# Layer 0's first feed-forward product with seven seven-product pairs instead of five, its weights and operands in order of use, and the groups around it divided

## The chip, the cores and the metric

The kernel runs on one core of one Trainium2 chip. The metric is the time of one execution in microseconds, as the device takes it; the time before is 2281.53 us, the median of three runs (2276.98 to 2283.56). A core has a matrix engine (TensorE, PE in the rows), a vector engine (DVE), a scalar engine (ScalarE, ACT), GpSimd (POOL) and SyncE (SP). Here SP issues the loads of weights, and POOL issues transfers that add one block of memory to another.

## The reference

Two layers of a recurrent trunk are computed on 512 time steps of width 1024, in single precision. Shortened:

```python
for i in range(DEPTH):                        # DEPTH = 2
    h = rmsnorm(x, norm1_g[i]);  z = h @ w_in[i] + b_in[i]
    # branch A: mLSTM with 4 heads; branch B: retention with 4 heads of q, k 256, v 512
    merged = sigmoid(gm) * (y_m @ w_bm[i]) + sigmoid(gr) * (y_r @ w_br[i])
    x = x + merged @ w_out[i]
    h2 = rmsnorm(x, norm2_g[i])
    x = x + square(relu(h2 @ w_ff1[i] + b_ff1[i])) @ w_ff2[i] + b_ff2[i]     # 1024 -> 4096 -> 1024
    h3 = rmsnorm(x, norm3_g[i])
    x = x + sigmoid(h3 @ w_pe_gate[i]) * (p[i] @ w_pe[i])
return rmsnorm(x, final_g)
```

## The kernel before

Activations lie transposed, features on the 128 partitions and the 512 time steps along the columns. Every product is made three times over: each operand is split into a high part and a low remainder, and high·high, high·low and low·high are summed (lines L502 to L504 for plain units, L557 to L559 for pairs). ScalarE makes the high part (L321), DVE the low one (L322), of weights as of activations.

A weight reaches TensorE in two forms. A **plain unit** ("T8") is one tile of 128 output columns: 24 matmuls of 512 columns, results named `l0f` in the feed-forward. A **pair** makes two such tiles by a seven-product scheme (Strassen's): the time steps are halved into 256 columns, and products P1 and P5 use the weight piece A, P6 and P2 piece B, P3 and P7 piece C, P4 piece D, twelve matmuls of 256 columns each, 84 in all. Its names are `l0f11` or `l0o10`, and its banks a, b and c. P4 is deferred: it runs inside the next unit, at the `flush()` behind that unit's P5 (or at the place that the unit has for it). The pieces A, B, C hold 1024 columns and D 512. They are sums of weight blocks. Most sums are made ahead in memory by POOL's adding transfers (L379), which are paced by a credit: each unit of work adds a share of its time (`SHARE`, from the third branch gate of layer 0 on `LATER`), each transfer takes off `STEP` = 1.13 us, and none is issued while the credit is negative. In layer 0 the sum in the second half of piece B of some groups and the one for D are made on DVE (for D, L484); in layer 1's first product all come from memory. Raw weights are loaded by SP into four buffers (`wr`), and the split pieces have three buffers; both are filled in one fixed order, the order of the units and within a unit that of `parts_of`: A, C, B, D.

The **feed-forward** has four groups b of 1024 hidden values. The first product of a group has four units "f" (b, p) of 256 hidden values: a pair where `FPAIRS` names it, else two plain units. What comes out is scaled on DVE (L1518), passed through relu and square on ScalarE (L1519, L1520) and split into quarters (`pair_quarters`: `hh`, `hl`, 128x768), and three sums of it on DVE (L652 to L654) are split as the last operand part (128x1024). The second product of the group has four pairs "o" (b, p), which use all four f units of their group; their products are added to `x` on DVE (L1554, L1556), and a bank is written again only behind such an addition. `ff_order` puts the first f unit of the next group between the last f unit of a group and its four o pairs. At the end of the feed-forward the embedding product (`l1pe`) takes this place, before `o30`.

In the retention branch, head after head, `attend` multiplies the decayed scores with the values in four slices j of 128 rows, slice j summing over j + 1 blocks of three matmuls. Before it lies the pair that makes the next head's key (`brk`), so that its deferred P4 is run at the `flush()` behind the first slice. This P4 needs a sum on DVE (L643) first.

A list scheduler with priorities sets the final order on each engine; queues are in order on SP and POOL.

## Time and profile before

| What | Value |
|---|---|
| runs, median (range) | 2281.53 us (2276.98 to 2283.56) |
| profiled execution, its span | 2280.06 us, 2278.3 us |
| granted TensorE clock | 0.999 |
| TensorE busy | 2263.4 us (99%) |
| DVE, ScalarE, POOL busy | 1747.5, 1281.5, 605.5 us |
| feed-forward of layer 0 | from about 757 to 1097 us |

Times of instructions are counted from the start of the span. A row of the timeline gives start, duration, engine, line, operation, the written tile, the tiles read, and in brackets the idle time ahead of it with the instruction that ended it. A window's row gives, for each engine, the busy time and in brackets the instructions, in the order PE, weight loads, DVE, ACT, POOL; then the granted clock, the busy share of the transfer engines and GB/s.

### The profile page before, as it was taken

The page shows a single profiled execution, that of the slowest core. Times are in us where ns is not written, and L with a number is a line of the kernel's source. Part 1 is how long each engine was busy: PE and PEld are TensorE (multiplying, and loading weights), DVE is VectorE, ACT ScalarE, POOL GpSimd, SP SyncE. Part 2 cuts the span into 40 slices and gives each one's busy share as a digit, 9 for nine tenths or more (in the row PEclk, how much of TensorE's full clock was granted, in tenths as well). Part 3 has the DMA queues.
Part 4 walks back from the last instruction along what each step waited for, and adds up shares of the span by engine and source line. Part 5 has one row for each costly group of instructions (what it writes and reads, how often), then busy time and mean ns, then how long its engine had stood idle before and what let it go on. Part 6 is the DMA issues. An engine that isn't in the chain of part 4 may idle for free.

```text
span 2278.3 us, 36390 instructions
## 1 busy us (share of the span) xinstructions
PE 2263.4 (99%) x13532; PEld 2009.3 (88%) x13532; DVE 1747.5 (77%) x2680; ACT 1281.5 (56%) x1881; POOL 605.5 (27%) x952
## 2 busy tenths in 40 slices
...
GB/s 215 189 192 176 246 224 223 222 232 216 236 231 267 222 229 228 238 238 222 227 220 197 185 178 244 240 210 223 239 216 219 248 265 217 256 239 231 249 159 60
DMA packets 185889, 499.32 MB, mean 219 GB/s; under 512 B 26400, under 2 KB 26784, under 8 KB 185712
## 3 DMA queue, kind: packets, MB, share of 16 engines
...
## 4 chain that ended last, share of the span: by engine, by line
PE 90%; DVE 5%; ACT 2%; issue 1%; DMA 1%; POOL 0%; SPq 0%; DVEq 0%; ACTq 0%; POOLq 0%
PE l0f L502 2%; PE l0f L503 2%; PE l0f L504 2%; PE l0br L502 1%; PE l0br L503 1%; PE l1br L502 1%; PE l1br L503 1%; PE l1br L504 1%; PE l0br L504 1%; DVE w_B L322 1%; PE l0pg L502 1%; PE l0pg L504 1%; PE l1bm L503 1%; PE l0bm L503 1%; PE l0bm L502 1%
## 5 line engine op out<-in xcount | busy, mean ns | idle before, releaser
L322 DVE TENSOR_TENSOR w<-wr,w 128x1024 fp32r<-128x1024 f32 (+1 forms) x193 | 234.3, 1217 | 47.6 <-ACT w L321 45.3
L321 ACT ACTIVATE w<-wr 128x1024 fp32r<-128x1024 f32 (+1 forms) x193 | 199.7, 1041 | 122.3 <-issue 28.5
L321 ACT ACTIVATE w_B<-wr 128x1024 fp32r<-128x1024 f32 x123 | 130.5, 1061 | 148.5 <-PE l1bm L504 13.1
L322 DVE TENSOR_TENSOR w_B<-wr,w_B 128x1024 fp32r<-128x1024 f32 x123 | 150.2, 1222 | 52.5 <-ACT w_B L321 52.3
L321 ACT ACTIVATE w_C<-wr 128x1024 fp32r<-128x1024 f32 x75 | 79.3, 1058 | 63.4 <-issue 9.5
L322 DVE TENSOR_TENSOR w_C<-wr,w_C 128x1024 fp32r<-128x1024 f32 x75 | 92.5, 1234 | 28.6 <-ACT w_C L321 28.6
L322 DVE TENSOR_TENSOR w_A<-wr,w_A 128x1024 fp32r<-128x1024 f32 x75 | 91.7, 1223 | 15.6 <-ACT w_A L321 14.6
L321 ACT ACTIVATE w_A<-wr 128x1024 fp32r<-128x1024 f32 x75 | 79.0, 1053 | 39.6 <-DMA wr<-wpairs 8.8
L321 ACT ACTIVATE w_t<-wr 128x1024 fp32r<-128x1024 f32 x56 | 59.4, 1060 | 62.7 <-PE l0g2va L610 6.3
L321 ACT ACTIVATE w_D<-wr 128x512 fp32r<-128x512 f32 x75 | 47.3, 631 | 67.3 <-DVE wr L484 18.3
L322 DVE TENSOR_TENSOR w_t<-wr,w_t 128x1024 fp32r<-128x1024 f32 x56 | 68.3, 1222 | 21.2 <-ACT w_t L321 20.6
L502 PE MATMUL l0f<-l0n2h,w 128*128 128x512 f32 x176 | 68.8, 391 | 0.0
L503 PE MATMUL l0f<-l0n2l,w 128*128 128x512 f32 x176 | 68.7, 390 | 0.0
L504 PE MATMUL l0f<-l0n2h,w 128*128 128x512 f32 x176 | 68.6, 390 | 0.0
L322 DVE TENSOR_TENSOR w_D<-wr,w_D 128x512 fp32r<-128x512 f32 x75 | 51.7, 689 | 14.1 <-ACT w_D L321 13.7
L379 POOL DMA_DIRECT2D s30t<-wpairs x24 | 16.8, 701 | 88.7 <-PE l1o20a L559 8.7
L504 PEld LDWEIGHTS l0f<-l0n2h,w 128*128 128x128 f32 x176 | 33.1, 188 | 6.9
L502 PEld LDWEIGHTS l0f<-l0n2h,w 128*128 128x128 f32 x176 | 33.1, 188 | 6.6
L503 PEld LDWEIGHTS l0f<-l0n2l,w 128*128 128x128 f32 x176 | 33.1, 188 | 6.5
L502 PE MATMUL l1f<-l1n2h,w 128*128 128x512 f32 x96 | 37.6, 392 | 0.0
L503 PE MATMUL l1f<-l1n2l,w 128*128 128x512 f32 x96 | 37.5, 390 | 0.0
L504 PE MATMUL l1f<-l1n2h,w 128*128 128x512 f32 x96 | 37.4, 390 | 0.0
...
## 6 DMA issues: line engine op xcount, KB each, us to landing
...
```

The source lines that it names most:

```text
L321: a = ac.activation(hi_ap, src, AF.Copy)
L322: return a, ve.tensor_sub(lo_ap, src, hi_ap.bitcast(F32))
L379: dma = gp.dma_start(piece(g, x, p, q), piece(g, MADE[x][a], p, q), max_dma_last_dim=4096, **kw)
L502: te.matmul(o, sh, mh, start=first, stop=False)
L503: te.matmul(o, sh, ml, start=False, stop=False)
L504: cur["mm"] = te.matmul(o, sl, mh, start=False, stop=last)
```

## The change

Five edits, made together:

1. `FPAIRS` of layer 0 names seven f units instead of five, so two units that were two plain ones each become pairs, and others change place: (0,2), (1,1), (1,2), (2,1), (2,2), (3,1), (3,2) for (1,1), (1,3), (2,1), (2,3), (3,1). Layer 1 keeps its ten.
2. Where the first f unit of the next group is plain, which is so for all three in layer 0 and none in layer 1, `ff_order` divides it: its first plain unit ("fa") goes ahead of two o pairs, its second one with the split of the operands ("fb") behind them, then come the other two.
3. Pieces of feed-forward pairs are split, and loaded, in the order A, B, C, D in which their products use them. Other pairs keep A, C, B, D.
4. `attend` begins with slice 1 where a deferred product is pending, and flushes behind that one: heads 0 and 2 of each layer.
5. `LATER` is .76 instead of .75. The adding transfers become 682 instead of 670.

```diff
--- before.py
+++ after.py
@@ -77,18 +77,21 @@
 SLACK = 64
 
 
-def ff_order():
+def ff_order(i):
 
     seq = [("f", 0, p) for p in range(4)]
     for b in range(3):
-        seq.append(("f", b + 1, 0))
-        seq += [("o", b, p) for p in range(4)]
+        o = [("o", b, p) for p in range(4)]
+        if (b + 1, 0) in FPAIRS[i]:
+            seq += [("f", b + 1, 0)] + o
+        else:
+            seq += [("fa", b + 1, 0)] + o[:2] + [("fb", b + 1, 0)] + o[2:]
         seq += [("f", b + 1, p) for p in range(1, 4)]
     return seq, [("o", 3, p) for p in range(4)]
 
 
 
-FPAIRS = (((1, 1), (1, 3), (2, 1), (2, 3), (3, 1)), ((0, 2), (1, 0), (1, 1), (1, 3), (2, 0), (2, 1), (2, 3), (3, 0), (3, 1), (3, 2)))
+FPAIRS = (((0, 2), (1, 1), (1, 2), (2, 1), (2, 2), (3, 1), (3, 2)), ((0, 2), (1, 0), (1, 1), (1, 3), (2, 0), (2, 1), (2, 3), (3, 0), (3, 1), (3, 2)))
 
 
 PRODUCTS = {"P1": ("A", 0, 0), "P5": ("A", 1, 4), "P2": ("B", 0, 2), "P6": ("B", 1, 5), "P3": ("C", 0, 6),
@@ -109,17 +112,22 @@
 HALVES = [(WIDE[x][0], u) for x, u in TURNS]
 
 SOON = ("w_in", 0, CGM + 2 * P)
-STEP, SHARE, LATER = 1.13, 0.75, 0.75
+STEP, SHARE, LATER = 1.13, 0.75, 0.76
 TIME = {"PAIR": (9.9, 3.9), "WIDE": (5.45, 2.7), "FULL": (9.9, 5.0)}
 
 
 def parts_of(u):
 
-    return {"PAIR": list(PIECE), "WIDE": HALVES}.get(u[0], [0])
+    pair = "ABCD" if u[0] == "PAIR" and is_ff(u[1]) else "ACBD"
+    return {"PAIR": list(pair), "WIDE": HALVES}.get(u[0], [0])
 
 
 
 READY = {"P1": 2, "P4": 2, "P5": 3, "P2": 4, "P6": 4, "P3": 4, "P7": 5}
+
+
+def is_ff(g):
+    return g[1][0] == "f"
 
 
 def is_wide(g):
@@ -237,15 +245,15 @@
         for kind, b, p in seq:
             if (b, p) in FPAIRS[i] and kind == "f":
                 pair(f"fp{b}", [q for c, q in FPAIRS[i] if c == b].index(p))
-            elif kind == "f":
-                t8("w_ff1", b * 1024 + 256 * p)
-                t8("w_ff1", b * 1024 + 256 * p + P)
+            elif kind[0] == "f":
+                for d in {"fa": (0,), "fb": (1,)}.get(kind, (0, 1)):
+                    t8("w_ff1", b * 1024 + 256 * p + d * P)
             else:
                 pair(f"ff{b}", p)
 
-    pairs(ff_order()[0])
+    pairs(ff_order(i)[0])
     u.append(("PE", 0))
-    pairs(ff_order()[1])
+    pairs(ff_order(i)[1])
     u.append(("PE", 1))
     full("w_pe_gate")
     return u
@@ -401,7 +409,10 @@
 
     order = [(n, x) for n, u in enumerate(units) for x in parts_of(u)]
     place = {x: k for k, x in enumerate(order)}
-    loads = [(n, x) for n, x in order if full(n) or x not in ("D", ("t4", 0), ("t4", 1))]
+    loads = []
+    for n, u in enumerate(units):
+        ls = "ACBD" if u[0] == "PAIR" and not has_t2(u[1]) else parts_of(u)
+        loads += [(n, x) for x in ls if full(n) or x not in ("D", ("t4", 0), ("t4", 1))]
     raws, pieces, kept = {}, {}, {}
     formed = {}
 
@@ -447,6 +458,14 @@
         at["prep"] += 1
         fill_raws()
 
+        g = units[n][1] if x in list("ABCD") else None
+
+        def t2_sum():
+            if not has_t2(g):
+                ve.tensor_tensor(raws[n, "B"][:, Q:], kept.pop((n, "A"))[:, Q:], raws[n, "C"][:, :Q], OP.add)
+
+        if x == "B" and is_ff(g):
+            t2_sum()
         w = Q if x == "D" else UN
         pl = cur["last"] if n >= NU - LAST else wpool
         kw = {"tag": "d", "bufs": 1} if x == "D" else {"tag": "l", "bufs": LAST} if pl is not wpool else {
@@ -459,7 +478,7 @@
         out_ = [both[:, o + a * w:o + a * w + w] for a in range(1 if gates else 2)]
         r = formed.pop((n, x), None)
         if r is None:
-            r = raws.pop((n, x))
+            r = raws[n, x]
         if gates:
             z = out_[0]
             gp.memset(z.bitcast(F32), 0.0)
@@ -472,13 +491,13 @@
         else:
             in_order("prep", *split(r[:, :w], *out_))
         pieces[n, x] = out_
-        if full(n) or not wide and x in ("A", "C") and has_t2(units[n][1]):
+        if x == "C" and not is_ff(g):
+            t2_sum()
+        raws.pop((n, x), None)
+        if full(n) or x == "C" or x == "A" and has_t2(g):
             pass
         elif x == "A" or wide and x[0] == "t2":
             kept[n, x] = r
-        elif x == "C":
-
-            ve.tensor_tensor(raws[n, "B"][:, Q:], kept.pop((n, "A"))[:, Q:], r[:, :Q], OP.add)
         elif x == "B":
 
             ve.tensor_tensor(r[:, :Q], r[:, :Q], r[:, Q:], OP.add)
@@ -858,13 +877,14 @@
 
     def attend(nm, pt, vh, vl, c0, n, num, each=None):
         ph, pl, offs = pt
-        for j in range(NT):
+        slices = (1, 0, 2, 3) if later else range(NT)
+        for j in slices:
             o = ps(f"{nm}a{j}")
             for i in range(j + 1):
                 s = slice(offs[i] + (j - i) * P, offs[i] + (j - i + 1) * P)
                 mm3(o[:, :n], ph[:, s], pl[:, s], vh[i][:, c0:c0 + n], vl[i][:, c0:c0 + n], i == 0, i == j)
             ac.activation(num[:, j, :], o[:, :n], AF.Copy)
-            if j == 0:
+            if j == slices[0]:
                 flush()
             if each:
                 each(j)
@@ -1507,7 +1527,9 @@
         cur["own"] = "new"
         hid = {}
 
-        def ff1(b, p):
+        begun = []
+
+        def ff1(b, p, part=False):
 
             nm = f"l{i}f{b}{p}"
             hid[b, p] = [cur["ff"].tile([P, 7 * S], F32R, name=f"l{i}h{a}{b}{p}", tag=f"h{a}", bufs=5) for a in "hl"]
@@ -1537,9 +1559,17 @@
                 evac(1, o1)
             else:
                 evac(0, o)
-                evac(1, t8(n2.act, f"{nm}1"))
-            pair_quarters(st, *hid[b, p])
-            pair_operand(nm, st, *hid[b, p])
+
+            def second():
+                if b or p:
+                    evac(1, t8(n2.act, f"{nm}1"))
+                pair_quarters(st, *hid[b, p])
+                pair_operand(nm, st, *hid[b, p])
+
+            if part:
+                begun.append(second)
+            else:
+                second()
 
         def tile3(c):
             n3.tile(c, x[c])
@@ -1578,10 +1608,13 @@
 
             run_pair(f"l{i}o{b}{p}", [parts(k) for k in range(4)], done)
 
-        first, rest = ff_order()
+        first, rest = ff_order(i)
         for kind, b, p in first:
             if kind == "o":
                 ff2(b, p)
+                continue
+            if kind == "fb":
+                begun.pop()()
                 continue
             if (b, p) == (3, 1):
                 pth, ptl = [cur["ff"].tile([P, 2, T], F32R, name=f"l{i}pt{a}", tag=f"h{a}", bufs=5) for a in "hl"]
@@ -1589,7 +1622,8 @@
                     t = tmp(f"l{i}ptr{k}")
                     nc.scalar.dma_start(t, ins["pT"][i, k])
                     split(t, pth[:, k, :], ptl[:, k, :])
-            ff1(b, p)
+            ff1(b, p, kind == "fa")
+        assert not begun
         ns_pool.release()
         n2_pool.release()
         n3_pool = phase(f"n3{i}", act_side)
```

What moves on the engines, at three places. First TensorE in layer 0's retention, head 0, around the deferred product of head 1's key (`l0r1brka`, piece `w51_D`); `l0r0a0` and `l0r0a1` are slices 0 and 1. Before:

```order
L559 MATMUL l0r1brka_3918<-l0xsh6_1371,w51_C_3890 128x256
L502 MATMUL l0r0a0_4045<-l0r0vh0_2629,l0r0ph_3747 128x512
L503 MATMUL l0r0a0_4045<-l0r0vl0_2633,l0r0ph_3747 128x512
L504 MATMUL l0r0a0_4045<-l0r0vh0_2629,l0r0pl_3748 128x512
L502 MATMUL l0r0a1_4081<-l0r0vh0_2629,l0r0ph_3747 128x512
L557 MATMUL l0r1brka_3918<-l0xnh1_1052,w51_D_3935 128x256
L558 MATMUL l0r1brka_3918<-l0xnl_386,w51_D_3935 128x256
```

With the change:

```order
L578 MATMUL l0r1brka_3921<-l0xsh6_1374,w51_C_3893 128x256
L521 MATMUL l0r0a1_4048<-l0r0vh0_2632,l0r0ph_3750 128x512
L522 MATMUL l0r0a1_4048<-l0r0vl0_2636,l0r0ph_3750 128x512
L523 MATMUL l0r0a1_4048<-l0r0vh0_2632,l0r0pl_3751 128x512
L521 MATMUL l0r0a1_4048<-l0r0vh1_2633,l0r0ph_3750 128x512
L522 MATMUL l0r0a1_4048<-l0r0vl1_2637,l0r0ph_3750 128x512
L523 MATMUL l0r0a1_4048<-l0r0vh1_2633,l0r0pl_3751 128x512
L576 MATMUL l0r1brka_3921<-l0xnh1_1055,w51_D_3938 128x256
L577 MATMUL l0r1brka_3921<-l0xnl_389,w51_D_3938 128x256
```

Six matmuls of slice 1 stand ahead of the deferred product, where three of slice 0 and the first of slice 1 stood.

Second, DVE ahead of `o10`, the first o pair of group 1 in layer 0. `l0hl13` is the operand of the group's last f unit, `l0f20st` the next group's first, `w107` (with the change `w105`) the pieces of `o10`. Before, with its piece C split four rows ahead of these:

```order
L322 TENSOR_TENSOR l0hl13_8754<-l0f13st_8755,l0hh13_8753 128x1024
L1518 TENSOR_TENSOR l0f20st_8864<-l0f201_8934,l0n2rb_7721 128x512
L322 TENSOR_TENSOR w107_B_8975<-wr197_8843,w107_B_8975 128x1024
L484 TENSOR_TENSOR wr197_8843<-wr197_8843 128x512
L652 TENSOR_TENSOR l0f20st_8864<-l0f20st_8864 128x512
L322 TENSOR_TENSOR l0hl20_8863<-l0f20st_8864,l0hh20_8862 128x768
L653 SCALAR_TENSOR_TENSOR l0f20st_8864<-l0f20st_8864 128x256
L322 TENSOR_TENSOR w107_D_8998<-wr197_8843,w107_D_8998 128x512
L654 SCALAR_TENSOR_TENSOR l0f20st_8864<-l0f20st_8864 128x256
L1556 TENSOR_TENSOR l0x1_7211<-l0x1_7211,l0o10c_9001 128x256
```

With the change:

```order
L1540 TENSOR_TENSOR l0f13st_8843<-l0f131_8913,l0n2rb_7728 128x512
L330 TENSOR_TENSOR w105_B_8956<-wr196_8822,w105_B_8956 128x1024
L503 TENSOR_TENSOR wr196_8822<-wr196_8822 128x512
L671 TENSOR_TENSOR l0f13st_8843<-l0f13st_8843 128x512
L330 TENSOR_TENSOR l0hl13_8842<-l0f13st_8843,l0hh13_8841 128x768
L672 SCALAR_TENSOR_TENSOR l0f13st_8843<-l0f13st_8843 128x256
L673 SCALAR_TENSOR_TENSOR l0f13st_8843<-l0f13st_8843 128x256
L1540 TENSOR_TENSOR l0f20st_8951<-l0f200_8960,l0n2rb_7728 128x512
L330 TENSOR_TENSOR w105_C_8994<-wr197_8845,w105_C_8994 128x1024
L330 TENSOR_TENSOR l0hl13_8842<-l0f13st_8843,l0hh13_8841 128x1024
L330 TENSOR_TENSOR w105_D_9015<-wr196_8822,w105_D_9015 128x512
L1586 TENSOR_TENSOR l0x1_7215<-l0x1_7215,l0o10c_9018 128x256
```

Piece B stands ahead of C, the evacuation and the operand of f13 stand between and behind them, and the operand sums of f20 (L652 before) are no longer here. TensorE in the same place, from the tenth matmul of `o10`'s second product on, with the change:

```order
L576 MATMUL l0o10c_9018<-l0hh13_8841,w105_A_8910 128x256
L576 MATMUL l0o10a_8997<-l0hh10_8041,w105_B_8956 128x256
L577 MATMUL l0o10a_8997<-l0hl10_8042,w105_B_8956 128x256
L578 MATMUL l0o10a_8997<-l0hh10_8041,w105_B_8956 128x256
L576 MATMUL l0o10a_8997<-l0hh11_8587,w105_B_8956 128x256
L577 MATMUL l0o10a_8997<-l0hl11_8588,w105_B_8956 128x256
L578 MATMUL l0o10a_8997<-l0hh11_8587,w105_B_8956 128x256
L576 MATMUL l0o10a_8997<-l0hh12_8707,w105_B_8956 128x256
L577 MATMUL l0o10a_8997<-l0hl12_8708,w105_B_8956 128x256
L577 MATMUL l0o10c_9018<-l0hl13_8842,w105_A_8910 128x256
L578 MATMUL l0o10c_9018<-l0hh13_8841,w105_A_8910 128x256
L578 MATMUL l0o10a_8997<-l0hh12_8707,w105_B_8956 128x256
```

Eight matmuls of the third product (piece B) are now ahead of the last two of the second, which read `l0hl13`'s and `l0hh13`'s last part.

Third, DVE ahead of layer 1's `f10`, whose pieces are `w234` (with the change `w232`). Before:

```order
L653 SCALAR_TENSOR_TENSOR l1f02st_19187<-l1f02st_19187 128x256
L322 TENSOR_TENSOR w234_C_19362<-wr432_19229,w234_C_19362 128x1024
L654 SCALAR_TENSOR_TENSOR l1f02st_19187<-l1f02st_19187 128x256
L322 TENSOR_TENSOR l1hl02_19186<-l1f02st_19187,l1hh02_19185 128x1024
L1518 TENSOR_TENSOR l1f03st_19296<-l1f031_19365,l1n2rb_19089 128x512
L322 TENSOR_TENSOR w234_B_19409<-wr433_19275,w234_B_19409 128x1024
```

With the change:

```order
L672 SCALAR_TENSOR_TENSOR l1f02st_19310<-l1f02st_19310 128x256
L330 TENSOR_TENSOR w232_B_19485<-wr434_19352,w232_B_19485 128x1024
L673 SCALAR_TENSOR_TENSOR l1f02st_19310<-l1f02st_19310 128x256
L330 TENSOR_TENSOR l1hl02_19309<-l1f02st_19310,l1hh02_19308 128x1024
L1540 TENSOR_TENSOR l1f03st_19419<-l1f031_19488,l1n2rb_19212 128x512
L330 TENSOR_TENSOR w232_C_19532<-wr435_19398,w232_C_19532 128x1024
```

B and C have changed places; the rest stays.

## The prediction

> **What bounds the kernel now.** I read the busy totals first, then the shares of the chain that ended last, then the layer-0 feed-forward stretch by windows, and last the matmuls and their waits in order of time.
>
> ```profile
> PE 2263.4 (99%) x13532; PEld 2009.3 (88%) x13532; DVE 1747.5 (77%) x2680; ACT 1281.5 (56%) x1881; POOL 605.5 (27%) x952
> PE 90%; DVE 5%; ACT 2%; issue 1%; DMA 1%; POOL 0%; SPq 0%; DVEq 0%; ACTq 0%; POOLq 0%
> ```
>
> TensorE is busy for 2263.4 of 2278.3 us, so time is saved by issuing fewer or cheaper matmuls, or by closing short stalls. The 15 us of unbusy time understate the stalls: the end of a matmul is modelled, so a gap after it can be swallowed by its record. I therefore take spacings between first matmuls, not busy sums.
>
> ```profile
> 851.00:893.00 42.00, 42.00 (x277) 38.28 (x276) 30.75 (x42) 28.16 (x42) 10.33 (x16) 1.00 0.82 228
> sum 340.00, PE 337.95 PEld 312.89 DVE 264.68 ACT 201.35 POOL 89.88; mean PE 42.24 PEld 39.11 DVE 33.09 ACT 25.17 POOL 11.23
> ```
>
> In the 340 us of layer 0's feed-forward (the sum is over its eight windows, 757 to 1097), DVE is busy 264.7 us and idle 75, ScalarE idle 139, at a granted clock of 1.00. Other engines have room on average; the question is order.
>
> **The change, part 1: two more pairs.** A plain unit is one weight tile, 24 matmuls of 512 columns; a pair makes two tiles with 84 matmuls of 256. First the plain units' window (192 matmuls, eight units), then the starts of the products around:
>
> ```profile
> 769.90:813.38 43.48, 43.48 (x192) 35.82 (x191) 7.34 (x6) 6.03 (x6) 0.00 (x0) 1.00 0.82 211
> 813.39 0.28 PE L557 MATMUL l0o00a<-l0hh,w_A 128*128 128x256 f32 x1
> 832.10 0.28 PE L557 MATMUL l0o02a<-l0hh,w_A 128*128 128x256 f32 x1
> 841.62 0.28 PE L557 MATMUL l0o03a<-l0hh,w_A 128*128 128x256 f32 x1
> 851.14 0.28 PE L557 MATMUL l0f11a<-l0n2h,w_A 128*128 128x256 f32 x1
> 872.98 0.28 PE L557 MATMUL l0f13a<-l0n2h,w_A 128*128 128x256 f32 x1
> 893.47 0.28 PE L557 MATMUL l0o10a<-l0hh,w_A 128*128 128x256 f32 x1
> 912.97 0.28 PE L557 MATMUL l0o12a<-l0hh,w_A 128*128 128x256 f32 x1
> 942.38 0.40 PE L502 MATMUL l0f<-l0n2h,w 128*128 128x512 f32 x1
> 975.18 0.28 PE L557 MATMUL l0o20a<-l0hh,w_A 128*128 128x256 f32 x1
> 994.42 0.28 PE L557 MATMUL l0o22a<-l0hh,w_A 128*128 128x256 f32 x1
> 1051.62 0.28 PE L557 MATMUL l0o30a<-l0hh,w_A 128*128 128x256 f32 x1
> 1069.93 0.28 PE L557 MATMUL l0o32a<-l0hh,w_A 128*128 128x256 f32 x1
> 2175.42 0.28 PE L557 MATMUL l1o30a<-l1hh,w_A 128*128 128x256 f32 x1
> 2194.20 0.28 PE L557 MATMUL l1o32a<-l1hh,w_A 128*128 128x256 f32 x1
> ```
>
> A plain unit is 43.48/8 = 5.44 us. A pair is 9.52 (832.10 to 841.62 to 851.14), so a product of 12 matmuls is 1.36 and a matmul .113. Each replacement saves 10.88 − 9.52 = 1.36, two of them 2.7. From 851.14 to 872.98 lie f11's seven products, the one deferred from o03 and f12's two plain units: 9.52 + 1.36 + 10.88 = 21.76, and the trace has 21.84, so .08 goes to switching the size. The new sequence switches about as often; I charge .1 in all. **Term: −2.6.**
>
> It hands work to the others. A pair needs three pieces of 1024 columns and one of 512 for two pieces of 1024, one sum for D and two evacuation sums. By DVE rows shown below (1.22 a split of 1024 columns, .69 the sum of 512, .42 the sum of 256) that is 1.5 × 1.22 + .69 + 2 × .42, some 3.4 us more on DVE per pair, 7 us for both, against the 75 idle; without this cover they would cost up to their whole 7. ScalarE gets about as much against 139 idle. SP loads three pieces where it loaded two, and GpSimd issues six more sum steps per pair (part 5). That adjacent pairs can run without stalls shows in layer 1:
>
> ```profile
> 2138.63 0.28 PE L557 MATMUL l1f31a<-l1n2h,w_A 128*128 128x256 f32 x1
> 2157.67 0.40 PE L502 MATMUL l1f<-l1n2h,w 128*128 128x512 f32 x1
> ```
>
> Two pairs, f31 and f32, take 19.04, exactly 2 × 9.52. They load D where layer 0 sums it on DVE, which is the .69 each that stays a risk.
>
> On the price of short matmuls the trace has a spacing of .113 for 256 columns, weight load included, since every matmul has its own load and 84 of them fit in 9.52. The Trainium skill, "TensorE: Matmul & The Clock Gate", section "Part 3: Packing small matmuls", says that a weight load overlaps running matmuls only when its row group differs; these loads all fill the 128 rows, so by that sentence they would not overlap, and this trace disagrees. The same page ("LDWEIGHTS") puts a load of 128 columns at about 107 ns; by it a pair would have some 6 ns of slack per matmul, or, unoverlapped, last an estimated 84 × (.113 + .107) = 18.5 us.
>
> **Part 2: stalls at the start of the second product's stage.** Behind each group of f units come four o pairs that need the group's squared hidden values. From the first pair's start to the third's lie 13 products (the second pair's deferred one comes later), 17.68 us at 1.36. Measured: o00 18.71, o10 19.50, o20 19.24, o30 18.31, layer 1's o30 18.78. The losses are 1.03, 1.82, 1.56, .63 and 1.10. The waits in them (last column) are mostly w_B or the x update behind which a bank is reused:
>
> ```profile
> 816.45 0.35 PE L557 MATMUL l0o00a<-l0hh,w_B 128*128 128x256 f32 x1 [0.15 <-DVE l0x L1554]
> 896.94 0.39 PE L559 MATMUL l0o10a<-l0hh,w_B 128*128 128x256 f32 x1 [0.34 <-DVE w_B L322]
> 900.74 0.38 PE L557 MATMUL l0o10c<-l0hh,w_C 128*128 128x256 f32 x1 [0.43 <-DVE l0x L1556]
> 978.67 0.39 PE L559 MATMUL l0o20a<-l0hh,w_B 128*128 128x256 f32 x1 [0.35 <-DVE w_B L322]
> 982.47 0.39 PE L557 MATMUL l0o20c<-l0hh,w_C 128*128 128x256 f32 x1 [0.42 <-DVE l0x L1556]
> 1938.09 0.39 PE L559 MATMUL l1f10a<-l1nsh,w_B 128*128 128x256 f32 x1 [0.44 <-DVE w_B L322]
> 2179.05 0.39 PE L559 MATMUL l1o30a<-l1hh,w_B 128*128 128x256 f32 x1 [0.36 <-DVE w_B L322]
> ```
>
> w_B is late because DVE splits w_C first, though products two blocks later use it, and then the last operand. Use order puts B ahead. The divided group also puts 5.44 us of a plain unit between the group's last f unit and the first o pair, as the embedding product does now in layer 1 (2169.98 to 2175.42). I walk o10 in the new order, 0 being the end of f13's second plain unit, with DVE's rows:
>
> ```profile
> 2169.98 0.39 PE L502 MATMUL l1pe<-l1pth,w 128*128 128x512 f32 x1
> 2171.45 0.69 DVE L1518 TENSOR_TENSOR l1f33st<-l1f,l1n2rb 128x512 f32<-128x512 f32 x1
> 895.66 1.22 DVE L322 TENSOR_TENSOR w_B<-wr,w_B 128x1024 fp32r<-128x1024 f32 x1
> 896.92 0.69 DVE L484 TENSOR_TENSOR wr<-wr 128x512 f32<-128x512 f32 x1
> ```
>
> The evacuation starts at 1.47 (2171.45 − 2169.98) and ends at 2.1; w_B 3.3; D's sum 3.9; three operand sums and the operand's first part to 6.2 (estimates in proportion to these columns); the next group's evacuation 6.8; w_C 8.0; the operand's last part 9.1. TensorE reaches what needs that last part after 5.44 (the plain unit) + 1.36 + ten matmuls + the eight of w_B that are now moved ahead, 18 × .113: 8.8. So w_B no longer waits and some .3 is left there; with the x update's wait, about .5 of o10's 1.8. Of the old losses .3 at o10 and layer 1's o30 is the slow spacing counted in part 4. I take −.5 at o00, −1.0 at o10, −1.05 at o20, −.55 at o30, −.7 at layer 1's o30, and −.75 at layer 1's f10 (the row's wait of .44 and an estimate of .3 for the restart, less than the ratio of wait to loss at o10). **Term: −4.55**, bounds 0 (the waits only move) and −6.9 (the five losses and .75).
>
> **Part 3: attention.** With a deferred product pending, the second slice goes first: six matmuls lie ahead of the flush, where now there are three and one of the next slice.
>
> ```profile
> 387.03 0.40 PE L502 MATMUL l0r0a<-l0r0vh,l0r0ph 128*128 128x512 f32 x1
> 387.11 0.42 DVE L643 TENSOR_TENSOR l0r1brky<-l0r1brka,l0r1brky 128x256 f32<-128x256 f32 x1
> 387.58 0.39 PE L557 MATMUL l0r1brka<-l0xnh,w_D 128*128 128x256 f32 x1 [0.15 <-DVE l0r1brky L643]
> 393.70 0.69 DVE L322 TENSOR_TENSOR l0r1kl<-l0r1brku,l0r1kh 128x512 fp32r<-128x512 f32 x1
> 394.99 0.39 PE L502 MATMUL l0r1s<-l0r1qh,l0r1kh 128*128 128x512 f32 x1
> ```
>
> The flush waits for DVE's sum that ends at 387.53. Now 387.03 to 387.58 is .55 where a 512-column matmul takes .227: .32 lost, and the product after it runs 1.49 against 1.38, .11. The fourth matmul starts at 387.03, so six are through at 387.03 + 3 × .227 = 387.71, after that sum: the wait is covered. The scores at 394.99 would come .43 earlier, 394.56, when their first k operand (393.70 + .69 = 394.39) is done. It is two heads in two layers: 4 × .43. **Term: −1.7**, bounds −.5 (the scores wait instead) and −1.9.
>
> **Part 4: spacing after a stall.** From 912.97 to 942.38 are 21 products in 29.41, 1.40 each instead of 1.36, until the stage changes; layer 1's end has the same. Some 27 + 24 products, at .04, are 2.0 us. If a stall sets this off, fewer stalls remove some; I take half. **Term: −1.0**, bounds 0 and −2.0.
>
> **Part 5: new waits.** The pairs f02 and f11–f12 put DVE's sums and GpSimd's 12 more steps into fuller stretches: **+.4**, bounds 0 and +2. The share .76 is to start the sums in time; the rows are a matmul of layer 0's third branch gate, from where on that share holds, the last sum, and the first load from the block that it completes:
>
> ```profile
> 598.11 0.39 PE L609 MATMUL l0g2vb<-w_B,l0xnh 128*128 128x512 f32 x1
> 2148.78 0.79 POOL L379 DMA_DIRECT2D s30t<-wpairs  x1 [7.47 <-PE l1f31a L559]
> 2155.93 0.44 SPq L432 DMA_DIRECT2D wr<-s30t  x1
> ```
>
> Sum and load are 7.15 us apart. Twelve steps at the planner's 1.13 us (a constant of the kernel) are 13.6 us of its credit, and .01 more of the 1551 us between the first two rows gives 15.5: it comes out even, so 0.
>
> **Sum**: −2.6 − 4.55 − 1.7 − 1.0 + .4 = −9.45. The profiled execution is 2280.06 (span 2278.3 and 1.8 around it), 1.5 under the median 2281.53. So span 2268.8, execution 2270.6, median **2272.1**.
>
> **The rivals.**
>
> *Waits only move* (chance .25). The walk above leaves the operand's last part .3 behind TensorE; with one DVE instruction more ahead of it each o stage loses 1.1 to 1.8 as now. For: DVE's order is crowded, 31 of 42 us. Against: 5.44 us of cover. The total is then −9.45 + 3.1 (part 2's four in layer 0) + 1.0 (part 4) = −5.35: 2276.2; layer 1's two, which hang on B's place alone, stay gained.
>
> *Adjacent pairs bound by DVE* (.08). A pair asks some 10.9 us of DVE (3.5 × 1.22, .69 twice, evacuation and operand) against 9.52 of TensorE; in f11–f12, f21–f22, f31–f32 the 1.36 that each new pair saves is lost again: −9.45 + 2.7, 2274.8. Against it stands layer 1's 19.04.
>
> *The slow spacing takes over* (.05, the case that ends slower). If 1.40 holds not after stalls but wherever 256-column products run without a break, and longer runs of pairs keep it going, 23 pairs in layer 0 and 26 in layer 1 pay 49 × 7 × .04 = 13.7 instead of 2.0: −8.45 + 11.7 = +3.3, 2284.8. It decides from (8.45 + 2.0) / .28 = 37 such pairs on. Against: o02 to f11 keep 9.52.
>
> *Weight loads bind* (.01). Were loads not hidden and as long as the matmuls, each new pair would cost 84 × .113 = 9.5 more than counted: −9.45 + 19.0, 2291.1; all spacings above exclude it. It is the page's sentence on row groups worked out from rows.
>
> *Sums late* (.04). If the share doesn't make up for the steps, the last block comes 13.6 us later, 7.15 of which are spare: up to 6.4 us of waiting, 2278.5.
>
> **The numbers.** My forecast has .57. Below .3%, 6.8 us, no change can be told from this measurement, so faster means under 2274.7. The forecast's own range is 2268 to 2276; its greater part (.54), half of the DVE rival and a fourth of the first give .63. Same: the rest of these, late sums and half of the slow spacing, .30. Slower, .07: the other half, the loads, and .03 for what no row shows. Low: all gains at their bounds are −2.7 − 6.9 − 1.9 − 2.0 = −13.5, 2268.0, less the 2 us by which runs differ: 2266.5. High: moved waits with +2 in part 5, 2278.5, say 2279.
>
> **What would show it.** From f11 to f12 9.52; from o10 to o12 (or with the plain unit between) 17.7 to 18.3 apart from the inserted 5.44, with no w_B wait; layer 1's f10 and o30 without one; no gap ahead of w_D after r0 and r2's first slice. Waits for the hidden operand at o10, o20 of .5 or more show the first rival, f11 to f12 well over 9.52 the second, 9.80 per pair throughout the third. It is wrong if the o stages keep their losses, or if a load of a block of sums is on the chain.

## The result

Three series of the changed kernel were timed, each beside the kernel before on the same chip:

| series | changed, median (range), runs | before, median | ratio, 95% interval |
|---|---|---|---|
| first | 2274.3 us (2273.77 to 2279.89), 8 | 2280.59 | 0.9975 [0.9966, 0.9985] |
| second | 2277.34 us (2276.25 to 2279.76), 10 | 2280.72 | 0.9990 [0.9981, 0.9999] |
| third | 2275.26 us (2274.31 to 2276.96), 11 | 2280.06 | 0.9977 [0.9968, 0.9986] |

The change gains 0.1 to 0.25%, 3 to 6 us. All three intervals lie under 1, and all three ratios inside the .3% that the prediction called no change. Forecast were 2272.1 us and a gain of 9.45; 2274.3 lies in the range of 2266.5 to 2279, but the forecast's own case was too high in its gain by 3 to 6 us, and the likeliest class, faster by over .3%, didn't come true. (2274.3 is just under the line of 2274.7, but that line was drawn from three runs of the kernel before with a median of 2281.53; beside the eight of this series the gain is .25%.)

First the busy totals of the changed kernel's profiled execution (2274.38 us, span 2272.6):

```profile
PE 2258.5 (99%) x13604; PEld 2009.6 (88%) x13604; DVE 1754.1 (77%) x2690; ACT 1284.0 (56%) x1895; POOL 616.6 (27%) x964
```

The span is 5.7 us shorter. DVE has 6.6 us more, about the 7 that part 1 said, ScalarE 2.5 and POOL 11.1. Where TensorE's time went is in the starts of its products:

```profile
805.38 0.28 PE L576 MATMUL l0o00a<-l0hh,w_A 128*128 128x256 f32 x1
823.56 0.40 PE L521 MATMUL l0f<-l0n2h,w 128*128 128x512 f32 x1
848.75 0.28 PE L576 MATMUL l0f11a<-l0n2h,w_A 128*128 128x256 f32 x1
867.79 0.40 PE L521 MATMUL l0f<-l0n2h,w 128*128 128x512 f32 x1
885.55 0.28 PE L576 MATMUL l0o10a<-l0hh,w_A 128*128 128x256 f32 x1
904.30 0.39 PE L521 MATMUL l0f<-l0n2h,w 128*128 128x512 f32 x1
911.17 0.28 PE L576 MATMUL l0o12a<-l0hh,w_A 128*128 128x256 f32 x1
929.48 0.28 PE L576 MATMUL l0f21a<-l0n2h,w_A 128*128 128x256 f32 x1
966.27 0.28 PE L576 MATMUL l0o20a<-l0hh,w_A 128*128 128x256 f32 x1
984.63 0.39 PE L521 MATMUL l0f<-l0n2h,w 128*128 128x512 f32 x1
1046.61 0.28 PE L576 MATMUL l0o30a<-l0hh,w_A 128*128 128x256 f32 x1
1065.43 0.28 PE L576 MATMUL l0o32a<-l0hh,w_A 128*128 128x256 f32 x1
```

From the first o pair of a group to the plain unit behind the second are 13 products again, 17.68 us at 1.36. Now o00 takes 18.18 (18.71 before), o10 18.75 (19.50), o20 18.36 (19.24), and o30 18.82 (18.31 before, so .5 more). The adjacent pairs take 19.04 each time (848.75 to 867.79, and as long from 929.48): nothing is lost there. But a new loss stands behind the divided unit: from 911.17 to 929.48 are 13 products and 18.31 us. The view of waits by instruction, for TensorE between 800 and 1100 us, names the releasers (us in total, times, longest):

```profile
PE l0o30a L576 <- ACT l0o30b L582: 0.8, 1, 0.8
PE l0o02c L576 <- DVE l0x L1584: 0.3, 1, 0.3
PE l0o22c L576 <- DVE l0x L1586: 0.2, 1, 0.2
PE l0o12c L576 <- DVE l0x L1586: 0.2, 1, 0.2
PE l0o10c L577 <- DVE l0hl L330: 0.2, 1, 0.2
PE l0o20c L577 <- DVE l0hl L330: 0.2, 1, 0.2
```

No w_B is left in it; the last two rows are the operand's last part, and the second to fourth the x update behind which bank c is reused, now in the *third* o pair of a group. In group 0 DVE scales the result of the second half unit, makes three sums of it and splits its first part before it comes to that update, 5.3 us later:

```profile
830.63 0.69 DVE L1540 TENSOR_TENSOR l0f10st<-l0f,l0n2rb 128x512 f32<-128x512 f32 x1 [2.26 <-PE l0f L523]
835.91 0.48 DVE L1584 SCALAR_TENSOR_TENSOR l0x<-l0x,bc,l0o02c 128x256 f32<-128x256 f32 x1
```

In layer 1, f10 before, from its first matmul to its first on bank b:

```profile
1934.51 0.28 PE L557 MATMUL l1f10a<-l1n2h,w_A 128*128 128x256 f32 x1
1939.36 0.28 PE L557 MATMUL l1f10b<-l1n2h,w_B 128*128 128x256 f32 x1
```

And with the change, with o30 behind it:

```profile
1930.69 0.28 PE L576 MATMUL l1f10a<-l1n2h,w_A 128*128 128x256 f32 x1
1934.79 0.28 PE L576 MATMUL l1f10b<-l1n2h,w_B 128*128 128x256 f32 x1
2171.67 0.28 PE L576 MATMUL l1o30a<-l1hh,w_A 128*128 128x256 f32 x1
2189.41 0.28 PE L576 MATMUL l1o32a<-l1hh,w_A 128*128 128x256 f32 x1
```

4.85 us became 4.10, and layer 1's o30 to o32 17.74, from 18.78.

### The profile page after: what moved, and what is told of

It reads as the page before. It is cut to its first block, busy times and chain, and to the rows that moved or that the text cites. A ratio compares the mean times of both kernels' runs of the same rounds, so it can differ in the third digit from the quotient of the medians.

```text
span 2272.6 us, 36647 instructions
## 1 busy us (share of the span) xinstructions
PE 2258.5 (99%) x13604; PEld 2009.6 (88%) x13604; DVE 1754.1 (77%) x2690; ACT 1284.0 (56%) x1895; POOL 616.6 (27%) x964
## 3 DMA queue, kind: packets, MB, share of 16 engines
q8 instruction: 106, 1.74, 0.3%
## 5 line engine op out<-in xcount | busy, mean ns | idle before, releaser
L329 ACT ACTIVATE w<-wr 128x1024 fp32r<-128x1024 f32 (+1 forms) x189 | 195.3, 1041 | 114.8 <-issue 23.3
L330 DVE TENSOR_TENSOR w<-wr,w 128x1024 fp32r<-128x1024 f32 (+1 forms) x189 | 228.9, 1215 | 39.8 <-ACT w L329 37.9
L329 ACT ACTIVATE w_B<-wr 128x1024 fp32r<-128x1024 f32 x125 | 132.3, 1058 | 123.5 <-PE l0bm L523 13.1
L329 ACT ACTIVATE w_C<-wr 128x1024 fp32r<-128x1024 f32 x77 | 81.8, 1062 | 106.7 <-PE l0f L523 21.5
L329 ACT ACTIVATE w_A<-wr 128x1024 fp32r<-128x1024 f32 x77 | 81.2, 1054 | 40.8 <-issue 11.2
L329 ACT ACTIVATE w_t<-wr 128x1024 fp32r<-128x1024 f32 x56 | 59.4, 1062 | 66.6 <-issue 6.3
L329 ACT ACTIVATE w_D<-wr 128x512 fp32r<-128x512 f32 x77 | 48.4, 629 | 52.5 <-issue 4.4
L521 PE MATMUL l0f<-l0n2h,w 128*128 128x512 f32 x144 | 56.4, 391 | 0.0
L522 PE MATMUL l0f<-l0n2l,w 128*128 128x512 f32 x144 | 56.2, 391 | 0.0
L523 PE MATMUL l0f<-l0n2h,w 128*128 128x512 f32 x144 | 56.1, 390 | 0.0
L387 POOL DMA_DIRECT2D s31t<-wpairs x24 | 16.8, 700 | 87.4 <-PE l1f L523 9.5
L503 DVE TENSOR_TENSOR wr<-wr 128x512 f32<-128x512 f32 x51 | 35.1, 688 | 0.7
L387 POOL DMA_DIRECT2D s6t<-wwide x24 | 17.0, 710 | 61.4 <-PE l0g0va L629 20.8
L387 POOL DMA_DIRECT2D s25t<-wpairs x24 | 17.1, 711 | 60.6 <-PE l1g0va L629 16.9
```

Of the source, the lines that this page charges most:

```text
L329: a = ac.activation(hi_ap, src, AF.Copy)
L330: return a, ve.tensor_sub(lo_ap, src, hi_ap.bitcast(F32))
L387: dma = gp.dma_start(piece(g, x, p, q), piece(g, MADE[x][a], p, q), max_dma_last_dim=4096, **kw)
L503: ve.tensor_tensor(r[:, :Q], r[:, :Q], r[:, Q:], OP.add)
L521: te.matmul(o, sh, mh, start=first, stop=False)
L522: te.matmul(o, sh, ml, start=False, stop=False)
```

## The experiments

The runs of one kernel lie 3 to 9 us apart, so differences of 1 or 2 us are read in the profiles: for each stretch, the spacings of its matmuls less .227 us for each of 512 columns and .1133 for each of 256. Products that run throughout at 1.40 (in the second series also at 1.44) are counted apart and taken out. That gives these losses in us; "o0" are the pairs o00 and o01 of layer 0, "fb" the third and fourth pairs of groups 0, 1 and 2 together, "heads 0" and "heads 2" the deferred product and the scores of the next head in both layers.

| kernel | o0 | o1 | o2 | o30, o31 | fb | layer 1 f10 | layer 1 o30 | heads 0 | heads 2 | products at 1.40 |
|---|---|---|---|---|---|---|---|---|---|---|
| before | 1.00 | 1.48 | 1.57 | .77 | 0 | .77 | .67 | .98 | 1.24 | 54 |
| changed | .53 | .69 | .71 | 1.14 | 1.93 | .02 | .02 | 1.82 | .40 | 57 |
| changed, second series | .52 | .74 | .50 | .66 | 1.87 | .02 | .02 | 1.72 | .36 | about 40, and 40 at 1.44 |
| changed, third series | .51 | .50 | .70 | 1.32 | 1.84 | .02 | .02 | 1.70 | .35 | 43 |
| slices 0, 1, 2, 3 | .52 | .70 | .75 | 1.97 | 1.93 | .02 | .01 | .99 | 1.27 | 74 |
| undivided | .56 | .65 | .58 | 1.00 | 0 | .02 | .06 | 1.74 | .34 | 75 |
| undivided, third series | .62 | .63 | .61 | 2.19 | 0 | .02 | .02 | 1.88 | .34 | about 40 |
| A, C, B, D | 1.67 | 1.31 | 1.31 | .53 | 2.15 | .50 | .69 | 1.75 | .39 | 153 |
| second half last | .51 | 1.42 | 1.36 | .67 | .09 | .02 | .02 | 1.85 | .39 | 103 |
| only pairs and share | .68 | .60 | .70 | .58 | 0 | .54 | .74 | .98 | 1.26 | 48 |
| five pairs, moved | 1.03 | .69 | .73 | .63 | 0 | .70 | .70 | .98 | 1.26 | 42 |

**Attention's order undone.**

```diff
-        slices = (1, 0, 2, 3) if later else range(NT)
+        slices = range(NT)
```

> The changed kernel with attention's slices in the order 0, 1, 2, 3 again (part 3 undone). As forecast, part 3 is worth 1.7 us: four waits of .3 ahead of w_D come back and the time rises from 2274.3 to about 2276.0. The rival, read from the changed kernel's trace: in heads 0 the scores of the next head now wait .3 to .8 for its key, because DVE does the first slice's statistics ahead of the key's rotation, so that only heads 2 kept their .45. Then the scores' wait goes with the slices (l0r1s and l1r1s back to a loss of .13 from .94 and .78), and the whole is worth .4 to .9: 2274.7 to 2275.2.

2278.11 us (2276.98 to 2279.98), .9992 [.9982, 1.0001]. The median lies above both forecasts, but the heads' part came out as the rival had it: heads 0 fall from 1.82 to .99 and heads 2 rise from .40 to 1.27, together 2.26 against 2.22. In the heads the order of the slices is worth nothing. What it is worth stands behind them, in no column: the two gate units behind heads 0 (l0g0v, l1g0v) lose .44 here and .06 in the changed kernel, so the order gives .4 us, the lower end of the rival's .4 to .9. The five profiles with the old order lose .44 to 1.28 there (.71 before), the nine with the new one .06. The rest of the 3.5 us that this profiled execution (2277.89) has over the first of the changed kernel lies elsewhere, most of all in 17 more products at 1.40 (.7) and at o30 (.8), which the slices don't touch.

In head 0 the flush no longer waits, as forecast, and the scores begin .84 earlier; then the stretch to the gate's first matmul grows. TensorE's starts in the changed kernel:

```profile
387.30 0.28 PE L576 MATMUL l0r1brka<-l0xnh,w_D 128*128 128x256 f32 x1
394.15 0.39 PE L521 MATMUL l0r1s<-l0r1qh,l0r1kh 128*128 128x512 f32 x1
398.83 0.40 PE L627 MATMUL l0g0va<-w_B,l0xnh 128*128 128x512 f32 x1
```

DVE in the same place of the same kernel:

```profile
389.42 0.69 DVE L1199 BATCH_NORM_STATS2 l0r0st<-l0r0num 128x6 f32<-128x512 f32 x1
390.02 0.74 DVE L1173 SCALAR_TENSOR_TENSOR l0r1brku<-l0r1brky,bc,l0cos 128x512 f32<-128x512 f32 x1
393.99 0.69 DVE L330 TENSOR_TENSOR l0r1kl<-l0r1brku,l0r1kh 128x512 fp32r<-128x512 f32 x1
```

The scores take 4.68 us (394.15 to 398.83), where they took 3.87 before (394.99 to 398.86). DVE does the first slice's statistics (389.42) ahead of the next key's rotation; before, it did them behind the key's first low part, though the slice was as early. That low part ends at 394.68; before, at 394.39, although the key's last product had come later. The greater part of the loss is on ScalarE, though. It makes the high part of the key's second half, L321 before (the first row) and L329 with the change; there the split of the next head's values has come ahead of it, and TensorE waits (last row):

```profile
395.02 0.64 ACT L321 ACTIVATE l0r1kh<-l0r1brku 128x512 fp32r<-128x512 f32 x1 [1.43 <-DVE l0r1brku L1155]
395.48 0.63 ACT L329 ACTIVATE l0r1vh<-l0r1vl 128x512 fp32r<-128x512 f32 x1 [0.53 <-DMA l0r1vl<-rv_spill]
396.02 0.61 ACT L329 ACTIVATE l0r1kh<-l0r1brku 128x512 fp32r<-128x512 f32 x1
396.69 0.50 PE L521 MATMUL l0r1s<-l0r1qh,l0r1kh 128*128 128x512 f32 x1 [0.34 <-ACT l0r1kh L329]
```

The matmul ahead of this one takes .62 instead of .12, so about .5 of the .94 goes there. With the slices in the old order the key comes ahead of the values again (395.54 and 396.78). In heads 2 the scores lose .07 before and after, so their .42 each is kept.

**The group undivided.**

```diff
-        if (b + 1, 0) in FPAIRS[i]:
+        if True:
```

> The changed kernel with the next group's first unit whole again, ahead of all four o pairs (edit 2 undone). Theory: the division pays for the first two o pairs only through order, not cover, since the whole unit gave 10.9 us of cover and the half gives 5.4; and it costs .6 at the third and fourth pair of three groups (x update late behind the second half's evacuation). So the three losses at o02, o12, o22 (1.9 together) go, while the first two pairs lose again what DVE's evacuation and quarters of the whole unit cost them, .5 to 1.2 a group: the time within 1 us of 2274.3. The forecast's view, that the division is what closed the stalls at o10 and o20: they return to 1.5 to 1.8 each and the time rises by about 2 us, to 2276.3.

2276.15 us (2272.30 to 2279.15), .9981 [.9972, .9990]. The table answers it: the first two o pairs lose .56, .65 and .58 without the division, .53, .69 and .71 with it, so the division closes none of these stalls; and the 1.93 behind the second half are gone. The forecast's view falls, and the theory's fear that the first pairs would lose .5 to 1.2 more falls too. The time alone would have said the opposite: 2276.15 is what the forecast's view gave, 2276.3. But it is of another series than 2274.3 (the kernel before had 2279.74 beside it, not 2280.59), and the two intervals overlap; the three versions below were timed on one chip.

**Order A, C, B, D again.**

```diff
 def is_ff(g):
-    return g[1][0] == "f"
+    return False
```

> The changed kernel with the feed-forward pieces split and loaded in the order A, C, B, D again (edit 3 undone). If B's place alone made the w_B waits, they come back: l1f10 .75, the o stages of layer 0 .3 to .6 more each in o00, o10, o20, and layer 1's o30 1.1: +2.5 to +3.5 us, 2277 to 2278. The rival: layer 1 gets faster where the slow spacing (1.40 a product) that followed o10 there no longer starts, -1.2, and o30 of both layers gets back the .5 that it lost because w_C's split on ScalarE stands ahead of the copy of P1: then 2275 to 2276.

2278.13 us (2276.64 to 2281.76), .9996 [.9986, 1.0006]. w_B's waits are back: 1.1 in o0, .6 each in o1 and o2, .5 at layer 1's f10 and .7 at its o30, and o30 of layer 0 gets .6 back, which only the rival had said; the rival's other gains, at layer 1's o30 and in the slow spacing, didn't come. With the third and fourth pairs it is together 3.1 more. The 153 products at 1.40, 96 more than in the changed kernel's first profile, make its profiled execution (2281.76) slower by another 3.8.

**The second half behind all four pairs.**

```diff
-            seq += [("fa", b + 1, 0)] + o[:2] + [("fb", b + 1, 0)] + o[2:]
+            seq += [("fa", b + 1, 0)] + o + [("fb", b + 1, 0)]
```

> The changed kernel with the second half of the divided unit behind all four o pairs instead of behind two. If the new losses at o02 and o03 (.63, .63 and .63 in the three groups of layer 0) come from the second half's evacuation and operand standing on DVE ahead of the x update, no o pair stands behind them now and all go: -1.9 us, 2272.4. The rival, that any 13 products in a row of o pairs wait for x updates whatever stands between, keeps them: 2274.3; and if four o pairs in a row without a plain unit keep the slow spacing alive after o10, +.5.

2277.55 us (2273.84 to 2279.70), .9989 [.9980, .9999]. The new losses at the third and fourth pair go (.09 of 1.93), so it was the second half ahead of them that delayed the x update. But o1 and o2 now lose 1.4 each, where o10 and o20 wait for the last part of the hidden operand (.6 each in the view of waits, half for ScalarE and half for DVE), and the plain units wait 1.3 us for their weights. The work was moved to other stalls, and the gain of 1.9 didn't come.

**The changed kernel again**, unaltered.

> The changed kernel once more, unaltered. So far the runs of each kernel lie 3 to 7 us apart, and the products at 1.40 instead of 1.36 us were 51 in the profile of before, 55 in that of the changed kernel and 71 to 152 in three variants. If the slow spacing starts by chance in each execution, this profile has another number of slow products at other places, at the same order and the same stalls elsewhere (within .2 us per pair), and its time differs by .04 us times the difference. If the spacing were set by the order of the instructions, the slow stretches lie where they lay: 890, 1446, 2023.

The second series of the table above. The order of instructions is the same; the slow stretches are not. In the first profile o12 to o13 of layer 1 took 9.80, in this one 9.52, and o22 to o23 the other way round. The starts of o12 and o13 in the first profile:

```profile
2036.66 0.28 PE L576 MATMUL l1o12a<-l1hh,w_A 128*128 128x256 f32 x1
2046.46 0.28 PE L576 MATMUL l1o13a<-l1hh,w_A 128*128 128x256 f32 x1
```

Those in the second:

```profile
2038.74 0.28 PE L576 MATMUL l1o12a<-l1hh,w_A 128*128 128x256 f32 x1
2048.26 0.28 PE L576 MATMUL l1o13a<-l1hh,w_A 128*128 128x256 f32 x1
929.71 0.28 PE L576 MATMUL l0f21a<-l0n2h,w_A 128*128 128x256 f32 x1
939.79 0.28 PE L576 MATMUL l0f22a<-l0n2h,w_A 128*128 128x256 f32 x1
```

The last two rows show a third spacing: f21 takes 10.08, which is 1.44 a product, where it took 9.52 in the first profile. Two stretches of 20 products run like this, in groups 1 and 2 of layer 0, at a granted clock of 1.00 as everywhere. So where the slow spacing falls, and how slow it is, is not set by the order alone; it differs from execution to execution. The first profile has 57 products at 1.40, 2.3 us; this one about 40 at 1.40 and 40 at 1.44, some 4.8 us, and its span is 2.0 us longer. The stalls elsewhere are not quite the same either: o30 loses .66 instead of 1.14. The profiles of this study have 20 to 153 products at 1.40, .8 to 6.2 us. That is of the size of the spread of the runs, though it was not measured run by run.

**Undivided, with the statistics held behind the last slice.** The diff is shortened, and leaves out the edit of the undivided variant.

```diff
-            if each:
+            if each and slices[0] == 0:
                 each(j)
+        if each and slices[0]:
+            for j in slices:
+                each(j, copy)      # bn_stats of all but slice 3 ordered behind the last slice's copy
```

> The changed kernel without the divided group (edit 2 undone, which took 2 us less of stalls in the o stages), and with the statistics of heads 0 and 2 held behind the copy of the last slice, so that DVE rotates the next head's key first. Theory: the scores' wait in the two heads 0 falls from .94 and .78 to about .12, 1.5 us, so the stalls sum to about 24.5 us against 27.3 in the changed kernel, and, the slow spacing aside, the time is 3.5 us under the changed kernel's: about 2271, with runs from 2269 to 2276. The rival: the key's operand on ScalarE, not DVE, sets the scores' start, or the statistics, now late, hold up the gates: the wait shrinks by less than .4 or comes back in l0g0v, and the time is that of the variant without division alone, 2276.

2278.25 us (2272.64 to 2281.68), .9988 [.9979, .9998]. The theory failed in its cure: heads 0 lose 3.19, not less. DVE in the same place now does a piece's split where the statistics stood:

```profile
390.26 1.22 DVE L330 TENSOR_TENSOR w_t<-wr,w_t 128x1024 fp32r<-128x1024 f32 x1
392.00 0.74 DVE L1176 SCALAR_TENSOR_TENSOR l0r1brku<-l0r1brky,bc,l0cos 128x512 f32<-128x512 f32 x1
```

A piece's split of 1.22 and one of the query now stand ahead of the rotation, and delay the key more than the statistics' .69 did. And on ScalarE the values' split is still ahead of the key's second half (396.75 and 397.29), which holding the statistics back doesn't touch; so far the rival was right. To keep the gain of heads 0 both places would have to be kept free; that was not tried.

**One more matmul of 512 columns in each o pair** of the undivided variant.

```diff
+            if x == "P5" and name[2] == "o":
+                te.matmul(bank[b][:, 0:T], wh[:, 0:P], wl[:, 0:T], start=True, stop=True, skip_group_check=True)
```

> The changed kernel without the divided group, and with one additional matmul of 512 columns at the start of P5 of each of the 32 o pairs (its result is overwritten by the product after it; nothing else is altered). It costs 32 x .227 = 7.3 us. Every slow stretch so far began behind a stall of some tenths inside an o pair and ended at a matmul of 512 columns. If such a matmul ends the slow spacing, no stretch is longer than about 8 products, the slow products fall to under 30 in all, and the runs lie closer together than the 7 us of the variant without it. If the spacing is some state that only time or a longer stretch ends, there remain stretches of 17 to 36 products.

2280.81 us (2278.52 to 2283.77), 1.0005 [.9996, 1.0014]. A stretch of 36 products, from o10 to f22, runs at 1.40 across the additional matmuls:

```profile
910.57 0.28 PE L578 MATMUL l0o12a<-l0hh,w_A 128*128 128x256 f32 x1
920.60 0.28 PE L578 MATMUL l0o13a<-l0hh,w_A 128*128 128x256 f32 x1
```

10.03 is 9.80 and .23 for the additional matmul. One matmul of 512 columns does not end the slow spacing, and the runs came hardly closer together (5.3 us). What starts it and what ends it stays open; nearly all long stretches began behind a stall and ended where a unit of 512-column matmuls began.

**Only the pairs and the share.** The kernel before with the new row of `FPAIRS` and `LATER` .76.

> The kernel before with seven pairs in layer 0 at the new places and the share .76, and nothing else (edits 1 and 5 alone). Forecast for this part: -2.6 us of matmul spacing, and with the new waits of part 5 (+.4) -2.2; slow products apart, a span of about 2276. The o stages keep their old order and so their losses of .6 to 1.8. The rival that adjacent pairs are bound by DVE: f11 to f13 and f21 to f23 take more than 2 x 9.52 by 1 us or more and the span stays at 2278.

One run, 2275.53 us. The span is 2273.8, under the 2276 expected: beside the matmuls, the o stages lose .68, .60 and .70 instead of 1.00, 1.48 and 1.57, without division and in the old order of the pieces. The rival with DVE falls.

**Five pairs at the new places.**

```diff
-FPAIRS = (((1, 1), (1, 3), (2, 1), (2, 3), (3, 1)), ...
+FPAIRS = (((1, 1), (1, 2), (2, 1), (2, 2), (3, 1)), ...
```

> The kernel before, still with five pairs in layer 0, but with those of groups 1 and 2 at (1,1), (1,2), (2,1), (2,2) instead of (1,1), (1,3), (2,1), (2,3), so that the last f unit of both groups is plain as it is in the changed kernel. Theory: a pair as the last unit gives its last part, the deferred P4, only inside the following plain unit, so its operand comes some 6 us later; the place alone takes the losses of the first two o pairs of groups 1 and 2 from 1.47 and 1.57 to about .6 each: -1.8 us with not one matmul less, about 2278. The rival: the gain there in the run with seven pairs came from the number of pairs or from the new order of the loads; then o10 and o20 keep 1.4 or more.

2277.66 us (2275.65 to 2280.64), .9988 [.9979, .9997]. With not one matmul less, o10 to o12 takes 18.52 and o20 to o22 18.41, where the kernel before has 19.50 and 19.24:

```profile
893.07 0.28 PE L557 MATMUL l0o10a<-l0hh,w_A 128*128 128x256 f32 x1
911.59 0.28 PE L557 MATMUL l0o12a<-l0hh,w_A 128*128 128x256 f32 x1
```

Only the places of the pairs differ. A pair as the last f unit delivers its last quarter with its deferred product, inside the unit behind it; a plain unit delivers everything at its end. DVE's split of the operand's last part shows it, before (first row) and with the moved pairs:

```profile
893.92 1.23 DVE L322 TENSOR_TENSOR l0hl<-l0f13st,l0hh 128x1024 fp32r<-128x1024 f32 x1 [1.13 <-ACT l0hh L321]
889.27 1.22 DVE L322 TENSOR_TENSOR l0hl<-l0f13st,l0hh 128x1024 fp32r<-128x1024 f32 x1 [0.53 <-ACT l0hh L321]
```

Before, it starts .45 us behind the start of o10 (893.47), and w_B's split, which comes after it, 2.2 behind; with the moved pairs it starts 3.8 us ahead of o10 (893.07) and w_B's split 1.3 behind its start. The place alone closes 1.6 us of stalls, slow products apart.

**Three versions on one chip.** The pairs and the share alone, the undivided variant, and the full change, in this order:

> The kernel before with the seven pairs and the share .76 alone, to be timed beside the next two on one chip. From the first profile (span 2273.8 with 48 slow products, stalls 28.4): 2.6 from the matmuls and 2.1 from the o stages, so about 4.7 us under before: 2275.5 to 2276. If the other three edits add what the forecast gave them, this lies 5 us or more over the full change; if they add nothing, the intervals of the two overlap.

> The changed kernel without the divided group, on the same chip as the full change. From the profiles: 2.0 us less of stalls in the o stages of groups 0 to 2, the rest equal: 2 us faster than the full change in the median, if the slow spacing falls alike on both; the rival is that the slow spacing, 0 to 6 us an execution, hides it, and the two medians lie within 1.5 us.

> The changed kernel once more, for the three-way comparison. Its medians so far were 2274.3 and 2277.3, against 2280.6 and 2280.7. If the first was a lucky series, this lies near 2276 to 2277, .998 to .999 of before; the o stages' stalls (1.2 to 1.9 a group in groups 0 to 2) and the scores' waits (.9 and .8) are there again.

| version | median (range), runs | ratio, 95% interval |
|---|---|---|
| pairs and share | 2275.78 (2274.11 to 2280.24), 11 | .9985 [.9976, .9994] |
| undivided | 2273.37 (2270.73 to 2275.41), 6 | .9969 [.9958, .9981] |
| full change | 2275.26 (2274.31 to 2276.96), 11 | .9977 [.9968, .9986] |

Two edits, the pairs and the share, already come within the full change's interval. The undivided variant has the lowest median here, 1.9 us under the full change, as the profiles' 1.9 would have it; but the intervals overlap, and in its first series it had 2276.15 on another chip. It beats the kernel before; that it beats the full change is likely and not shown. Its profiled execution here (2275.41) is the slowest of its six and no faster than the full change's (2275.55): the 1.9 are gone there too, but o30 loses 2.19, against 1.00 in the undivided variant's first profile.

**A late sum in layer 1.** One more loss is in no column: in layer 1's first key pair the kernel before, and the five moved pairs, lose nothing; every kernel with seven pairs loses .5 to 1.5. The rows are the changed kernel's, DVE and TensorE:

```profile
1443.82 0.69 DVE L465 TENSOR_TENSOR wr<-wr,wr 128x512 f32<-128x512 f32 x1 [2.24 <-DMA wr<-wpairs]
1444.43 0.42 DVE L662 TENSOR_TENSOR l1r0brqy<-l1r0brqa,l1r0brqy 128x256 f32<-128x256 f32 x1
1444.90 0.38 PE L576 MATMUL l1r0brqa<-l1xnh,w_D 128*128 128x256 f32 x1 [0.63 <-DVE l1r0brqy L662]
```

DVE stands at a sum whose raw weights have not landed, and the sum that TensorE needs stands behind it in the queue. Of the transfers in the 16 us around it, the issues with their count, size and median time to landing are these with the change, from 1430 to 1446:

```profile
s23t<-wpairs POOLq DMA_DIRECT2D x4, 256.0 KB, 5.8
wr<-wpairs SPq DMA_DIRECT2D x3, 256.0 KB, 6.1
s24t<-wpairs POOLq DMA_DIRECT2D x3, 256.0 KB, 5.8
```

And before, from 1434 to 1450:

```profile
wr<-wpairs SPq DMA_DIRECT2D x3, 256.0 KB, 4.6
s23t<-wpairs POOLq DMA_DIRECT2D x2, 256.0 KB, 5.0
s23t<-s23t POOLq DMA_DIRECT2D x2, 256.0 KB, 4.4
```

Seven adding transfers stand where there were four, and the loads take 6.1 us instead of 4.6. The load that DVE waits for is issued as early as before by TensorE's place (both are 5.0 us earlier in the span), so it is the landing that is late. That the transfers slow it is read from this coincidence; and no run changed the share alone, so whether the share or the twelve more sums bring it about stays open.

## Why the prediction was right and wrong

Its range held, its forecast didn't: 9.45 us were promised and 5.7 came in the profiled execution. By its own steps:

- **Part 1, two more pairs, −2.6: right.** The spacings leave 2.6 us for it (5.7 less 3.1 by which all losses and slow products together shrank), the adjacent pairs take 19.04, and DVE's 7 us of work are hidden. The rivals of a DVE bound and of weight loads that bind are out. With the latter goes the sentence of the Trainium skill on row groups ("TensorE: Matmul & The Clock Gate", section "Part 3: Packing small matmuls"): in the changed kernel too 84 matmuls with a weight load each take 9.52 us.
- **Part 2, −4.55: the wrong step.** By the table, in which slow products are taken out, o00 −.47, o10 −.79, o20 −.86, o30 +.37, layer 1's f10 −.75 and its o30 −.65, together −3.15; then +1.93 behind the second half, so −1.2. The prediction's own sign of being wrong came, "if the o stages keep their losses": groups 0 to 2 lost 4.05 and lose 3.86. The walk for o10 was good in itself: "some .3 is left" at the operand's last part, and the row has .2. Two things were wrong with it. I asked what the half unit covers and not what its other half does: it puts an evacuation, three sums and the splits of an operand on DVE ahead of the x updates of the third pair. That wait was in the profile, at o10 and o20, with the same releaser (l0x L1556), and I counted it only where it stood. And I gave the credit to order and division; the runs give it, in groups 1 and 2, to the place of the pairs, which I used only for counting matmuls. The order B before C is worth .5 to .75 and .65 in layer 1, about as forecast; in layer 0 it does next to nothing in groups 0 to 2 when the group is undivided (.68, .60, .70 without, .56, .65, .58 with). At o30 it put ScalarE's split of w_C (1.04 us) ahead of the copy of P1, behind which bank a is reused: the wait of .8 <- ACT l0o30b in the waits above, forecast as .08 of loss left and measured as 1.14. The profiles with this order lose .66 to 2.2 there, those with the old one .5 to .8.
- **Part 3, −1.7: wrong in its size**, near its bound of −.5; that bound's "the scores wait instead" was the right mechanism. Heads 2 gave .84, heads 0 took .84 back, and what is left is the .65 that the gates behind heads 0 no longer lose (.4 when the slices alone are undone). I checked that the first key operand of the time before (394.39) would be in time, and took it as fixed; but its place in DVE's queue changed with the order, and the key's second half, which I didn't look at, fell behind the values' split on ScalarE.
- **Part 4, −1.0: wrong.** 54 slow products became 57. The premise that fewer stalls mean fewer of them isn't borne out: where they fall changes from execution to execution of one program.
- **Part 5, +.4: undersized.** Adjacent pairs cost nothing, where I looked for the price; in layer 1's key pair a late sum cost .8 (and .15 in the matmuls right behind the wait), where I did not. No engine waits for a load from the last block of sums in the changed kernel's three profiles, so that rival is out. (Its 7.15 us of spare time were misread: in the kernel before the first load from that block stands at 2154.55, 5.77 us behind the last sum, and with the change the first load stands ahead of the last sum, at 2150.80 and 2154.44, so the distance doesn't give the spare time.)

These terms make −2.6 − 1.2 − .65 + .1 + .95 = −3.4. The other 2.3 us of the profile's 5.7 have no term; 1.7 of it lies at these places: .4 at the start, .4 at o32 and o33, .5 and .4 in layer 1's o33 and o20. At the start the other two profiles of the changed kernel lose as much as the kernel before, or within .2 us of it. At o32 and o33 and at layer 1's o33 the five moved pairs, whose order there is that of before, lose as little as the changed kernel. That part was in the one profile of before and is not the change's. The second series, 3.4 us, would agree with that. So that 2274.3 came within 2.2 us of the forecast is in part luck.

One sum in the prediction is off: by its own numbers the lower bound is 2268.0 − 2 = 2266.0, not 2266.5, and the 2 us by which runs were said to differ are 6.6 in the three runs of the kernel before.

The rival that waits only move (2276.2) is nearest to what happened in kind; the waits moved to the third pair and to the scores, not to the operand. The DVE rival's 2274.8 is nearer in time to the first and third series, but its mechanism isn't there.
